# A two-layer decoder trunk: two squared blocks a layer taken pair by pair, the turn and the last stage rearranged

## The chip, the cores and the metric

One NeuronCore of one Trainium2 chip runs the whole kernel. The metric is the device time of one execution in microseconds, as the median of several runs. The profile is of one execution with its own time.

## What is computed

Two decoder layers over 256 rows of 2048 float32 values, weights streamed from HBM once. In words per layer (cut from the reference):

```python
a = rms_norm(x, n_mix_pre); proj = a @ w_in                  # 9760 columns
o_fox, o_nsa = fox_attention(...), nsa_attention(...)        # 8 + 8 heads of 128
mix = sigmoid(g_fox) * (o_fox @ w_up_fox) + sigmoid(g_nsa) * (o_nsa @ w_up_nsa)
x = x + rms_norm(mix @ w_out, n_mix_post)
a = rms_norm(x, n_ffn_pre)
h = (silu(a @ w_gate) * (a @ w_up)) @ w_down                 # hidden width 5632
x = x + rms_norm(h, n_ffn_post)
```

## The kernel before

The 256 rows are two halves of 128 (`t` = 0, 1). A float32 product is made as three TensorE products of rounded parts: high by high, high by low, low by high (`part`, `product`). The left operand is the transposed activation (`aT`, `hT`); the right operand is weights in units of 256 rows by 512 columns (432 in the first stage of a layer). A unit goes from HBM into one of 5 raw buffers by SP's DMA queue (`emit_raw`, L252), ScalarE rounds it to `wh` (L158) and VectorE subtracts that to give `wl` (L168): `split`. High and low parts live in 37 slots of 4 KB a partition, as do activations.

The program writes the order of each engine's instructions itself. `ensure(i)` is called ahead of each use of unit `i`: it emits splits up to `i`, and one more step of the next splits if the units alive stay within `room["slots"]` (set by `budget` and by the stages) and the look-ahead within `room["ahead"]`; with `room["slow"]` every second call does nothing more. `finish` gives slots back. `pump` after each unit advances one of up to two generators of side work (transposes, turns of the residual stream), which yield between their steps; `Once.need` drives one until it has yielded a key.

`chunk` makes 512 columns for both halves, unit by unit, half 0 and half 1 in turn. `skew=8` takes the last 8 units for half 0 first and then for half 1, so that half 0 is evacuated earlier; `on_t0` then starts its turn. `head=8` does the same with the first units.

`square_chunk` makes 512 columns of two weights (gate and up) or 1024 of one. Its first two pairs of units (`SEVEN = 2`) are taken with seven products in place of eight, over sums of blocks: `split_sums` makes the rounded sums in two steps (of 2 and 4 slot tiles), the left sums stand in `smh` and `sml`, and seven PSUM banks hold the products, each of three matmuls. With `together` the order is product by product, both pairs in each; without, pair by pair. `between` then combines the banks, and the remaining pairs follow in plain form. FFN blocks 2 to 10 of a layer are squared, with `together`; blocks 5 to 10 are the second part. `room["slots"]` is 14 in the down block ahead of block 5, and falls from 24 in block 5 to 14 in block 10 (L1281, L1368). The down products are squared too, pair by pair.

`tail` makes the last product of a stage (`out`, and the second part of `down`, which adds to partial sums `yg`), with `sum_evac`: add the partial sum (L604), square with row sums on ScalarE (L606), multiply by the norm's gains in place (L607). In `down` the first 1024 columns are one squared block of 12 pairs, then two chunks follow. `turn_gen` takes a half across to the next stage: the root from the row sums on POOL (`rstd_of`, L501 to L508), x plus scaled y in four pieces (L570), transposes into `aT` (`to_aT`), a copy of x to HBM. `end_gen` does the last stage and stores the output.

The program starts with `idle(6)`, six matmuls of zeros, while the first x comes in; `start_gen` transposes it.

Of the kernel before, what the change touches and what calls it, by code (L numbers as in the profile page):

```python
# [43 lines left out]
RAWS = 5  # L44
IDLE = (6, 1)
LAG = (3, 4)
KEPT = (1, 1)
ROOM_OUT = 10
ROOM_DOWN = 10

# [54 lines left out]
def trunk(ctx: ExitStack, tc: tile.TileContext, I: dict, consts: bass.AP, out: bass.AP):  # L105
# [68 lines left out]

    def load_x(src):
        xs = [[None, None], [None, None]]
        for t in range(2):
            for i in range(2):
                xs[t][i] = slot([128, 1024], F32, f"x{t}{i}")
                nc.sync.dma_start(xs[t][i], src[t * 128:(t + 1) * 128, i * 1024:(i + 1) * 1024])  # L180
        return xs

    gp = slot([128, 2, 128], F32, "gp")
# [254 lines left out]

    def square_chunk(pairs, lhs, sums, between, evac, before=None, together=True):

# [104 lines left out]
    def start_gen(t, xs, aT, rs, gcol):  # L545
        ss = small([128, 4], F32, "ss", 4)

        def rows(c):
            return xs[t][c // 2][:, (c % 2) * 512:(c % 2) * 512 + 512]

        for c in range(4):
            to_aT(aT, t, c, rows(c), gcol, True, t == 0 and c == 0)
            yield c
        for c in range(4):
            act.activation(junk, rows(c), AF.Square, accum_out=ss[:, c:c + 1])
            yield "sum"
        rs[t] = rstd_of(ss, "rs", True)
        yield "rs"

    def turn_gen(t, yg, ssy, xs, aT, rs, gcol, keep, lag):  # L560

        ry = rstd_of(ssy, "ry")
        yield "ry"
        ss = small([128, 4], F32, "ss", 4)

        def half(v, c):
            return v[t][c // 2][:, (c % 2) * 512:(c % 2) * 512 + 512]

        def add(c):
            dve.scalar_tensor_tensor(half(xs, c), half(yg, c), ry[:, 0:1], half(xs, c), op0=OP.mult, op1=OP.add)  # L570

        add(0)
        add(1)
        for _ in range(lag[t]):
            yield "add"
        for c in range(4):
            if c < 2:
                add(c + 2)
            to_aT(aT, t, c, half(xs, c), gcol)
            act.activation(junk, half(xs, c), AF.Square, accum_out=ss[:, c:c + 1])  # L580
# [8 lines left out]
    def end_gen(t, yg, ssy, xs):  # L589
        ry = rstd_of(ssy, "ry")  # L590
        for c in range(4):
            v = slice((c % 2) * 512, (c % 2) * 512 + 512)
            x, y = xs[t][c // 2][:, v], yg[t][c // 2][:, v]
            dve.scalar_tensor_tensor(x, y, ry[:, 0:1], x, op0=OP.mult, op1=OP.add)  # L594
            nc.sync.dma_start(out[0, t * 128:(t + 1) * 128, c * 512:(c + 1) * 512], x)
        yield "end"

    def sum_evac(yg, ssy, gb, c, partial):
        v = slice((c % 2) * 512, (c % 2) * 512 + 512)

        def go(t, p):
            y = yg[t][c // 2][:, v]
# [7 lines left out]
    def gain_rows(v):  # L610
        gb = [slot([128, 1024], F32, f"gb{i}") for i in range(2)]
        for i in range(2):
# [355 lines left out]
    def run_layer(l, P, aT, rs, turns, x_src, x_mid, x_next):  # L968
# [156 lines left out]


        xs = load_x(x_src)
        gb = gain_rows(I["norm_mix_post"][l])

# [10 lines left out]

        def tail(ids4, lhs, gb, xs, yg, partial, wait, gen):
            ssy = [small([128, 4], F32, "ssy", 4) for t in range(2)]
            turns = [None, None]

            def turn(t):
                turns[t] = Once(gen(t, yg, ssy[t], xs))
                waiting.append(turns[t])
# [3 lines left out]
            def between(ps):  # L1151

                y = [[yg[t][0][:, 512 * i:512 * i + 512] for i in range(2)] for t in range(2)]
                hu = staged([128, 2, 512], F32, "hu", 1)
# [8 lines left out]
                dve.tensor_tensor(y[1][1], y[1][1], hu[:, 0], op=OP.add)  # L1163

            for c in range(4):
                end = c == 3
                if ids4[c] is None:
                    continue
                if c == 2:
                    room["ahead"] = 11  # L1170
                if partial and c == 0:
                    ev = [sum_evac(yg, ssy, gb, i, partial) for i in range(2)]
                    square_chunk(ids4[0], lhs, lhs_s, between, lambda t, i, p: ev[i](t, p), wait, False)
# [11 lines left out]
        turns2 = tail(P["out"], lhs_m, gb, xs, y_rows(), False, wait_m,  # L1185
                      lambda t, yg, ss, xs: turn_gen(t, yg, ss, xs, aT2, rs2, g2, x_mid, LAG))
        del xs, gb
# [89 lines left out]
        def ffn(c):  # L1277
# [53 lines left out]

            square_chunk(P["ffn"][c], lhs_a2, lhs_s, between, evac)
            made_of(c, hb)
# [39 lines left out]
        hand_on()  # L1373
        xs = load_x(x_mid)
        gb = gain_rows(I["norm_ffn_post"][l])
        budget(ROOM_DOWN)
        if l + 1 < DEPTH:
            aT3, rs3 = [[None] * 4, [None] * 4], [None, None]
            g3 = (l + 1) * 16
            turns3 = tail(P["down"][1], lhs_h(b0), gb, xs, yg, True, wait_h(b0, b1),  # L1380
                          lambda t, yg, ss, xs: turn_gen(t, yg, ss, xs, aT3, rs3, g3, x_next, LAG))
            close_stage()
            return aT3, rs3, turns3
        tail(P["down"][1], lhs_h(b0), gb, xs, yg, True, wait_h(b0, b1), end_gen)
        drain()
# [69 lines left out]
```

## Time and profile before

| | |
|---|---|
| time, median of 3 runs | 2829.85 us (2827.48 to 2831.4) |
| the profiled execution | 2828.34 us, its span 2826.4 us |
| TensorE busy (matmul) | 2799.8 us, 99% of the span |
| VectorE, ScalarE, GpSimd (POOL) busy | 1937.1, 1409.2, 112.1 us |
| DMA | 547.04 MB, mean 194 GB/s |
| mean granted TensorE clock | 0.997 of full |

The span runs from the first to the last instruction of the profiled execution; its time has 1.9 us more. PE is TensorE, DVE VectorE, ACT ScalarE, SP SyncE's queue. Matmul ends are modelled and overlap the next start, so the distance from start to start says how long one takes in a stream. A bracket behind an instruction gives the idle time of its engine just before it and what ended it.

### The profile page before, as it was taken

The page shows a single profiled execution, that of the slowest core. Times are in us where ns is not written, and L with a number is a line of the kernel's source. Part 1 is how long each engine was busy: PE and PEld are TensorE (multiplying, and loading weights), DVE is VectorE, ACT ScalarE, POOL GpSimd, SP SyncE. Part 2 cuts the span into 40 slices and gives each one's busy share as a digit, 9 for nine tenths or more (in the row PEclk, how much of TensorE's full clock was granted, in tenths as well). Part 3 has the DMA queues.
Part 4 walks back from the last instruction along what each step waited for, and adds up shares of the span by engine and source line. Part 5 has one row for each costly group of instructions (what it writes and reads, how often), then busy time and mean ns, then how long its engine had stood idle before and what let it go on. Part 6 is the DMA issues. An engine that isn't in the chain of part 4 may idle for free. (4 is left out here: it accounts for less than half of the span.)

```text
span 2826.4 us, 35553 instructions
## 1 busy us (share of the span) xinstructions
PE 2799.8 (99%) x13134; PEld 2345.4 (83%) x13134; DVE 1937.1 (69%) x2485; ACT 1409.2 (50%) x1999; POOL 112.1 (4%) x190
## 2 busy tenths in 40 slices
PE   9999999999999999999999999999999999999998
PEld 8988888888888878878899888888888888788786
DVE  6666655556888788776666576655468886887755
ACT  6555554445554455454555455644465454555443
POOL 0100000001000000000011000000020000000000
PEclk9999999999999999999999999999999999999999
DMA  7674446575665565556566644455666655665564
GB/s 247 205 255 123 138 149 206 189 244 189 202 217 179 174 225 194 179 179 238 184 216 220 222 128 149 147 196 194 231 219 210 203 176 190 209 192 185 177 206 156
DMA packets 291807, 547.04 MB, mean 194 GB/s; under 512 B 17265, under 2 KB 59569, under 8 KB 291633
## 3 DMA queue, kind: packets, MB, share of 16 engines
q1 hardware_dynamic: 290000, 543.82, 58.6%
q8 instruction: 103, 1.69, 0.2%
q10 hardware_dynamic: 1632, 0.95, 0.1%
q14 instruction: 72, 0.58, 0.1%
HBM read 536.31 MB, written 8.39 MB: 193 GB/s over the span
## 5 line engine op out<-in xcount | busy, mean ns | idle before, releaser
L168 DVE TENSOR_TENSOR wl<-raw,wh 128x1024 fp32r<-128x1024 f32 (+1 forms) x912 | 1070.4, 1210 | 334.9 <-ACT wh L158 280.0
L158 ACT ACTIVATE wh<-raw 128x1024 fp32r<-128x1024 f32 (+1 forms) x1056 | 1059.3, 1044 | 459.2 <-DVE raw L272 129.2
L388 PE MATMUL acc<-wh,aT 128*128 128x512 f32 (+1 forms) x1534 | 597.9, 390 | 0.0
L390 PE MATMUL acc<-wh,aT 128*128 128x512 f32 (+1 forms) x1534 | 585.1, 381 | 0.9 <-DVE aT L542 0.9
L389 PE MATMUL acc<-wl,aT 128*128 128x512 f32 (+1 forms) x1534 | 584.8, 381 | 0.0
L435 PE MATMUL acc<-wh,aT 128*128 128x512 f32 x972 | 381.3, 392 | 0.0
L437 PE MATMUL acc<-wh,aT 128*128 128x512 f32 x972 | 378.8, 390 | 0.0
L436 PE MATMUL acc<-wl,aT 128*128 128x512 f32 x972 | 378.2, 389 | 0.0
L390 PEld LDWEIGHTS acc<-wh,aT 128*128 128x128 f32 x1534 | 287.9, 188 | 51.3 <-DVE aT L542 1.7
L388 PEld LDWEIGHTS acc<-wh,aT 128*128 128x128 f32 x1534 | 288.5, 188 | 44.0 <-issue 0.8
L389 PEld LDWEIGHTS acc<-wl,aT 128*128 128x128 f32 x1534 | 288.7, 188 | 41.5
L437 PEld LDWEIGHTS acc<-wh,aT 128*128 128x128 f32 x972 | 182.5, 188 | 38.4
L436 PEld LDWEIGHTS acc<-wl,aT 128*128 128x128 f32 x972 | 182.7, 188 | 37.0
L435 PEld LDWEIGHTS acc<-wh,aT 128*128 128x128 f32 x972 | 182.7, 188 | 36.8
L263 DVE TENSOR_TENSOR wl<-raw,wh 128x1024 fp32r<-128x1024 f32 x144 | 173.6, 1221 | 18.5 <-PE acc L436 9.2
L435 PE MATMUL acc<-wh,hT 128*128 128x512 f32 x452 | 176.9, 391 | 0.0
L437 PE MATMUL acc<-wh,hT 128*128 128x512 f32 x452 | 176.2, 390 | 0.0
L436 PE MATMUL acc<-wl,hT 128*128 128x512 f32 x452 | 175.9, 389 | 0.0
L388 PE MATMUL acc<-wh,oT 128*128 128x512 f32 x256 | 102.0, 399 | 0.0
L388 PE MATMUL acc<-wh,mixT 128*128 128x512 f32 x256 | 100.7, 393 | 0.0
L390 PE MATMUL acc<-wh,oT 128*128 128x512 f32 x256 | 99.9, 390 | 0.0
L390 PE MATMUL acc<-wh,mixT 128*128 128x512 f32 x256 | 99.7, 390 | 0.0
(333 smaller groups left out, 3295.7 us busy)
## 6 DMA issues: line engine op xcount, KB each, us to landing
raw<-in_w_in SPq DMA_DIRECT2D x224, 512.0 KB, 4.6
raw<-in_w_ffn_gate SPq DMA_DIRECT2D x176, 512.0 KB, 4.8
raw<-in_w_ffn_up SPq DMA_DIRECT2D x176, 512.0 KB, 4.6
raw<-in_w_ffn_down SPq DMA_DIRECT2D x176, 512.0 KB, 5.5
raw<-in_w_in SPq DMA_DIRECT2D x96, 432.0 KB, 4.4
raw<-in_w_out SPq DMA_DIRECT2D x64, 512.0 KB, 6.1
raw<-in_w_up_nsa SPq DMA_DIRECT2D x32, 512.0 KB, 4.7
raw<-in_w_up_fox SPq DMA_DIRECT2D x32, 512.0 KB, 4.6
```

The lines of the kernel that those rows point to most:

```text
L158: act.activation(o, i, AF.Copy, scale=1.0 if scale is None else scale)
L168: dve.tensor_tensor(lo, src, f32(hi), op=OP.subtract)
L263: dve.tensor_tensor(lo, src, f32(hi), op=OP.subtract)
L388: pe.matmul(ps[t][:, :n], ah, hi, start=first, stop=False)
L389: pe.matmul(ps[t][:, :n], ah, lo, start=False, stop=False)
L390: pe.matmul(ps[t][:, :n], al, hi, start=False, stop=end)
L435: pe.matmul(ps, ah, bh, start=first, stop=False)
L436: pe.matmul(ps, ah, bl, start=False, stop=False)
L437: pe.matmul(ps, al, bh, start=False, stop=last)
```

## The change

- FFN blocks 5 and 10 (the first and the last of the second part) go through `square_chunk` pair by pair (`together=False`).
- In `down`'s tail the multiplication by the gains is put off by one evacuation in the squared block; in the last chunk its result goes to a new tile `z`, and in the last layer half 1's go to PSUM banks. `skew` is 6 there (8 in `out`), `ROOM_DOWN` 9.
- The loads of x and of the gains move from before that squared block to its pair 5; the gains go into the tiles `smh` and `sml`, half 0's x into the tiles `wq`.
- The turn after `down` begins its first two adds in the step that makes the root (`prompt`); the turn after `out` does not.
- In the last stage of the program half 1's first quarter is scaled by ScalarE, added by GpSimd and stored from ScalarE's queue.
- `start_gen` has one more step between the second and third transposes; ten matmuls of zeros in place of six.

```diff
-IDLE = (6, 1)
+IDLE = (10, 1)
-ROOM_DOWN = 10
+ROOM_DOWN = 9
...
-    def square_chunk(pairs, lhs, sums, between, evac, before=None, together=True):
+    def square_chunk(pairs, lhs, sums, between, evac, before=None, together=True, load=None):
...
         for p in range(SEVEN, last + 1):
+            if load is not None and p == SEVEN + 3:
+                load()
...
             to_aT(aT, t, c, rows(c), gcol, True, t == 0 and c == 0)
             yield c
+            if c == 1:
+                yield "later"
...
+    def quarters(v):
+
+        return [[i[:, k:k + 512] for i in v[t] for k in (0, 512)] for t in range(2)]
...
+    def turn_gen(t, ys, ssy, xs, aT, rs, gcol, keep, prompt):
...
         ry = rstd_of(ssy, "ry")
-        yield "ry"
+        if not prompt:
+            yield "ry"
...
         add(0)
         add(1)
-        for _ in range(lag[t]):
+        for _ in range(LAG[t]):
             yield "add"
...
+    def end_gen(t, ys, ssy, xs):
         ry = rstd_of(ssy, "ry")
...
+        if t:
+
+            copy(act, ys[t][0], ys[t][0], ry[:, 0:1])
+            pool.tensor_tensor(x[0], ys[t][0], x[0], op=OP.add)
+            store(nc.scalar, 0)
+        for c in range(t, 4):
+            dve.scalar_tensor_tensor(x[c], ys[t][c], ry[:, 0:1], x[c], op0=OP.mult, op1=OP.add)
+            store(nc.sync, c)
         yield "end"
...
+    def sum_evac(ys, ssy, gb, c, partial, place):
...
             act.activation(junk, p, AF.Square, accum_out=ssy[t][:, c:c + 1])
-            dve.tensor_tensor(y, p, gb[c // 2][:, v], op=OP.mult)
+            ys[t][c] = place(t) or y
+
+            def times_gain():
+                dve.tensor_tensor(ys[t][c], p, gb[c // 2][:, v], op=OP.mult)
+            return times_gain
         return go
...
+            def place(c):
+
+                def of(t):
+                    if last and t and c:
+                        return bank(8 - c, "yb")
+                    return z[:, t] if partial and c == 3 else None
+                return of
+
             for c in range(4):
                 end = c == 3
+                if end and partial:
+                    z = slot([128, 2, 512], F32, "z")
...
+                    ev = [sum_evac(ys, ssy, gb, 0, True, place(0)), sum_evac(ys, ssy, gb, 1, True, place(1))]
+                    left = deque()
+
+                    def sums_of(t, i, p):
+                        left.append(ev[i](t, p))
+                        if len(left) > 1:
+                            left.popleft()()
+                    square_chunk(ids4[0], lhs, lhs_s, between, sums_of, wait, False, load)
+                    left.popleft()()
                 else:
-                    chunk(ids4[c], lhs, sum_evac(yg, ssy, gb, c, partial), skew=8 if end else 0,
+                    ev = sum_evac(ys, ssy, gb, c, partial, place(c))
+                    chunk(ids4[c], lhs, lambda t, p: ev(t, p)(), skew=0 if not end else 6 if partial else 8,
...
-            square_chunk(P["ffn"][c], lhs_a2, lhs_s, between, evac)
+            square_chunk(P["ffn"][c], lhs_a2, lhs_s, between, evac, together=c not in (b0, b1 - 1))
...
-        xs = load_x(x_mid)
-        gb = gain_rows(I["norm_ffn_post"][l])
+        xs, gb = [None, None], [None, None]
+
+        def load():
+
+            gb[:] = [staged([128, 1024], F32, nm, 1) for nm in ("smh", "sml")]
+            gain_rows(I["norm_ffn_post"][l], gb)
+            xs[:] = [[staged([128, 1024], F32, "wq") for i in range(2)], x_tiles(1)]
+            load_x(x_mid, xs)
+
         budget(ROOM_DOWN)
...
+                          lambda t, yg, ss, xs: turn_gen(t, yg, ss, xs, aT3, rs3, g3, x_next, True), load)
+            turns3[0].need("kept")
             close_stage()
```

## Rows read from the trace of the kernel before

**Rows 1.** The page, part 1: busy time and share of the span, each engine
```profile
PE 2799.8 (99%) x13134; PEld 2345.4 (83%) x13134; DVE 1937.1 (69%) x2485; ACT 1409.2 (50%) x1999; POOL 112.1 (4%) x190
```

**Rows 2.** The waits of PE: us in total, times, longest
```profile
PE acc L436 <- DVE wl L263: 9.8, 4, 2.8
PE acc L389 <- DVE wl L168: 0.9, 2, 0.4
```

**Rows 3.** The timeline at the start of blocks 5 and 10, layer 0
```profile
1015.39 0.40 PE L435 MATMUL acc<-wh,smh 128*128 128x512 f32 x1
1018.61 0.50 PE L436 MATMUL acc<-wl,smh 128*128 128x512 f32 x1 [2.11 <-DVE wl L263]
...
1233.07 0.40 PE L435 MATMUL acc<-wh,smh 128*128 128x512 f32 x1
1234.83 2.35 DVE L263 TENSOR_TENSOR wl<-raw,wh 128x1024 fp32r<-128x1024 f32 x2
1237.23 0.50 PE L436 MATMUL acc<-wl,smh 128*128 128x512 f32 x1 [2.78 <-DVE wl L263]
```

**Rows 4.** Windows of 20 us: busy (x), PEclk, DMA share, GB/s
```profile
1240.00:1260.00 20.00, 20.00 (x94) 16.56 (x93) 16.48 (x21) 9.49 (x11) 0.00 (x0) 1.00 0.57 185
2640.00:2660.00 20.00, 20.00 (x81) 16.29 (x82) 13.77 (x19) 6.89 (x9) 0.00 (x0) 0.86 0.47 153
2760.00:2780.00 20.00, 20.00 (x90) 16.57 (x89) 14.01 (x12) 11.69 (x11) 0.00 (x0) 1.00 0.95 325
```

**Rows 5.** The timeline as rows 0 to 127 turn, between the layers
```profile
1400.09 0.69 DVE L604 TENSOR_TENSOR yg<-acc,yg 128x512 f32<-128x512 f32 x1 [7.03 <-PE acc L390]
1401.78 0.68 POOL L504 TENSOR_SCALAR nw<-ssy,nw 128x1 f32<-128x1 f32 x1 [16.22 <-ACT junk L606]
1404.15 1.42 DVE L570 SCALAR_TENSOR_TENSOR x<-yg,ry,x 128x512 f32<-128x512 f32 x2 [1.83 <-POOL ry L508]
1405.34 0.60 PE L493 MATMUL tp<-ct,x 128*128 128x128 f32 x4
```

**Rows 6.** The timeline as rows 128 to 255 turn, between the layers
```profile
1410.82 1.05 DVE L168 TENSOR_TENSOR wl<-raw,wh 128x864 fp32r<-128x864 f32 x1
1415.47 0.68 DVE L604 TENSOR_TENSOR yg<-acc,yg 128x512 f32<-128x512 f32 x1
1417.91 1.38 POOL L505 TENSOR_TENSOR nw<-nw,warm 128x1 f32<-128x1 f32 x1
1421.47 0.66 PE L493 MATMUL tp<-ct,x 128*128 128x128 f32 x4 [0.53 <-DVE x L570]
1425.00 0.46 PE L390 MATMUL acc<-wh,aT 128*128 128x432 f32 x1 [0.86 <-DVE aT L542]
```

**Rows 7.** The timeline of DVE after the squared block of the tail
```profile
1348.77 0.69 DVE L607 TENSOR_TENSOR yg<-yg,gb 128x512 f32<-128x512 f32 x1 [0.85 <-ACT junk L606]
```

**Rows 8.** The timeline of PE in the first 15 us
```profile
1.17 2.74 PE L1413 MATMUL idle<-junk 128*128 128x512 bf16 x6 [1.17 <-DVE warm L189]
4.83 0.63 PE L493 MATMUL tp<-ct,x 128*128 128x128 f32 x4 [0.92 <-DMA x<-in_x]
14.69 0.95 PE L493 MATMUL tp<-ct,x 128*128 128x128 f32 x4 [1.12 <-DVE aT L542]
```

**Rows 9.** The timeline of the last stage
```profile
2816.18 0.69 DVE L604 TENSOR_TENSOR yg<-acc,yg 128x512 f32<-128x512 f32 x1 [4.07 <-PE acc L390]
2820.22 2.74 DVE L594 SCALAR_TENSOR_TENSOR x<-yg,ry,x 128x512 f32<-128x512 f32 x4 [1.81 <-POOL ry L508]
```

**Rows 10.** Groups of POOL by line and shape: busy, mean ns
```profile
L519 POOL TENSOR_TENSOR ropea<-kskw,ct 128x128 f32<-128x128 f32 x4 | 1.9, 463 | 108.2 <-ACT kskw L158 108.0
L520 POOL TENSOR_TENSOR ropeb<-kskw,ct 128x64 f32<-128x64 f32 x4 | 1.3, 326 | 0.0
L522 POOL TENSOR_TENSOR ropeb<-nq,ct 128x128 f32<-128x128 f32 x4 | 5.8, 1447 | 0.0
```

**Rows 11.** The waits of SyncE's DMA queue: us in total, times, longest
```profile
SPq L252 <- DVE wl L168: 1862.3, 885, 18.1
```

More of the change, by code (lines that the diff above doesn't have):

```diff
@@ L173, in trunk, with load_x, x_tiles @@
     x_in = I["x"][0]
-    def load_x(src):
-        xs = [[None, None], [None, None]]
+    def load_x(src, xs):
         for t in range(2):
             for i in range(2):
-                xs[t][i] = slot([128, 1024], F32, f"x{t}{i}")
                 nc.sync.dma_start(xs[t][i], src[t * 128:(t + 1) * 128, i * 1024:(i + 1) * 1024])
         return xs
+    def x_tiles(t):
+        return [slot([128, 1024], F32, f"x{t}{i}") for i in range(2)]
     gp = slot([128, 2, 128], F32, "gp")
@@ L578, in turn_gen @@
                 add(c + 2)
-            to_aT(aT, t, c, half(xs, c), gcol)
-            act.activation(junk, half(xs, c), AF.Square, accum_out=ss[:, c:c + 1])
+            to_aT(aT, t, c, x[c], gcol)
+            act.activation(junk, x[c], AF.Square, accum_out=ss[:, c:c + 1])
             yield c
@@ L587, in turn_gen, with store @@
         yield "rs"
-    def end_gen(t, yg, ssy, xs):
+    def end_gen(t, ys, ssy, xs):
         ry = rstd_of(ssy, "ry")
[L591 to L595, printed above, removed]
+        x = quarters(xs)[t]
+        def store(queue, c):
+            queue.dma_start(out[0, t * 128:(t + 1) * 128, c * 512:(c + 1) * 512], x[c])
+        if t:
[3 more added lines that the diff above has]
+        for c in range(t, 4):
+            dve.scalar_tensor_tensor(x[c], ys[t][c], ry[:, 0:1], x[c], op0=OP.mult, op1=OP.add)
+            store(nc.sync, c)
         yield "end"
-    def sum_evac(yg, ssy, gb, c, partial):
+    def sum_evac(ys, ssy, gb, c, partial, place):
         v = slice((c % 2) * 512, (c % 2) * 512 + 512)
         def go(t, p):
-            y = yg[t][c // 2][:, v]
+            y = ys[t][c]
             if partial:
@@ L606, in go, with gain_rows @@
             act.activation(junk, p, AF.Square, accum_out=ssy[t][:, c:c + 1])
-            dve.tensor_tensor(y, p, gb[c // 2][:, v], op=OP.mult)
-        return go
-    def gain_rows(v):
-        gb = [slot([128, 1024], F32, f"gb{i}") for i in range(2)]
+            ys[t][c] = place(t) or y
+            def times_gain():
+                dve.tensor_tensor(ys[t][c], p, gb[c // 2][:, v], op=OP.mult)
+            return times_gain
+        return go
+    def gain_rows(v, gb):
         for i in range(2):
@@ L1124, in run_layer @@
         close_stage()
-        xs = load_x(x_src)
-        gb = gain_rows(I["norm_mix_post"][l])
+        xs = load_x(x_src, [x_tiles(t) for t in range(2)])
+        gb = gain_rows(I["norm_mix_post"][l], [slot([128, 1024], F32, f"gb{i}") for i in range(2)])
         def lhs_m(t, kt):
@@ L1139, in y_rows, with tail @@
             return [[slot([128, 1024], F32, f"yg{t}{i}") for i in range(2)] for t in range(2)]
-        def tail(ids4, lhs, gb, xs, yg, partial, wait, gen):
+        def tail(ids4, lhs, gb, xs, yg, partial, wait, gen, load=None, last=False):
+            ys = quarters(yg)
             ssy = [small([128, 4], F32, "ssy", 4) for t in range(2)]
@@ L1145, in turn @@
             def turn(t):
-                turns[t] = Once(gen(t, yg, ssy[t], xs))
+                turns[t] = Once(gen(t, ys, ssy[t], xs))
                 waiting.append(turns[t])
@@ L1151, in between @@
             def between(ps):
-                y = [[yg[t][0][:, 512 * i:512 * i + 512] for i in range(2)] for t in range(2)]
+                y = ys
                 hu = staged([128, 2, 512], F32, "hu", 1)
@@ L1185, in run_layer @@
         turns2 = tail(P["out"], lhs_m, gb, xs, y_rows(), False, wait_m,
-                      lambda t, yg, ss, xs: turn_gen(t, yg, ss, xs, aT2, rs2, g2, x_mid, LAG))
+                      lambda t, yg, ss, xs: turn_gen(t, yg, ss, xs, aT2, rs2, g2, x_mid, False))
         del xs, gb
@@ L1380, in run_layer @@
             turns3 = tail(P["down"][1], lhs_h(b0), gb, xs, yg, True, wait_h(b0, b1),
-                          lambda t, yg, ss, xs: turn_gen(t, yg, ss, xs, aT3, rs3, g3, x_next, LAG))
+                          lambda t, yg, ss, xs: turn_gen(t, yg, ss, xs, aT3, rs3, g3, x_next, True), load)
+            turns3[0].need("kept")
             close_stage()
             return aT3, rs3, turns3
-        tail(P["down"][1], lhs_h(b0), gb, xs, yg, True, wait_h(b0, b1), end_gen)
+        tail(P["down"][1], lhs_h(b0), gb, xs, yg, True, wait_h(b0, b1), end_gen, load, True)
         drain()
```

8 lines of the change are left out of this document (2 added, 6 removed).

## The prediction

> **What bounds the kernel now.** I read the page first: TensorE is busy 99% of the span and no other engine comes near [rows 1]. The change adds four small matmuls and removes none, so it can win only where TensorE stands still, where its clock is low, and after its last matmul. The second view was therefore the list of what TensorE waits for: one wait carries most of it, the products of a squared block (L436) waiting for low halves that VectorE subtracts at L263, four times, 9.8 us [rows 2]. The third was the timeline at those four places: the first matmuls of FFN blocks 5 and 10, in both layers. In each the first product of pair 0 runs (three matmuls), then the same product of pair 1 begins and its second matmul waits [rows 3]. The fourth was a table of windows, for the granted clock: it is 1.00 after the stall of block 10 in layer 0, and 0.86 over 20 us after the same stall in layer 1 [rows 4]. The last was the timeline of the turn between the layers, the tail's evacuations, the start and the end [rows 5 to 9].
>
> **Blocks 5 and 10 (together=False).** Now both pairs are wanted within four matmuls. Matmuls in a block start 0.23 us apart (some 88 begin in the undisturbed window [rows 4]). Block 5: from its first matmul at 1015.39 to the released one at 1018.61 are 3.22 us for four starts, 0.92; lost 2.30. Block 10: 1233.07 to 1237.23, 4.16, lost 3.24 [rows 3]. The waits of both layers add up to twice these two (9.8 against 2.11 + 2.78 [rows 2, 3]), so the four cost 2 x 5.54 = 11.1 us. In the new order all seven products of pair 0, 21 matmuls or 4.83 us, stand ahead of pair 1. VectorE's queue there does not change: the second step of pair 1's split is emitted at the head of the block in both orders, by `ensure`, behind the same evacuations. In block 10 VectorE works on it from 1234.83 to 1237.18; pair 1's low half is first wanted at 1233.07 + 4.83 + 0.23 = 1238.1. In block 5 it is ready by 1018.6 and wanted at 1020.4 [rows 3]. So the cover is 0.9 us in block 10 and 1.8 in block 5, and the stalls go whole: **-11.1**. Bounds: 0 (another wait takes the place of each) and -11.1. What is late next: the sums in `between` start after product 1, with 9 matmuls (2.1 us) behind it in place of 18; the bank of product 1 is written again only 18 matmuls later still, so 6.2 us cover a copy and four adds of about 0.7 each (L604, one pass of 512 [rows 5]). `ensure` is called four times in the head in place of nine, but pair 0's slots come free 4.8 us after the start, and pair 2 is wanted after 42 matmuls, 9.7 us. I cost both at nothing.
>
> **The clock.** [...] It follows the stall of block 10 in layer 1, so without the stall I take **-2.8**; bounds 0 and -2.8. The stall of equal length in layer 0 was not followed by it. [...]
>
> **Evacuations of the tail's squared block.** The multiplication by the gains (L607) overwrites what ScalarE still squares, so VectorE waits 0.85 us each of four times [rows 7], and the splits queued behind it make TensorE wait 0.4 us once a layer, 0.9 in all [rows 2]. With the multiplication put off by one evacuation, VectorE needs 8 passes of 0.69, 5.5 us, without those waits, and the splits come 2 us or more earlier: **-0.9**, bounds 0 and -0.9.
>
> **Loads of x and gains.** They move from before the tail's squared block to its sixth pair, on SP's queue among the weights; six loads of 512 KB at 325 GB/s [rows 4] take 9.7 us. Behind them wait the weight loads, and for these the splits. SP stands waiting for a free raw buffer for 1862 us of the span [rows 11], so five loads (and up to four split units) lie ahead: nine units of 12 matmuls at 0.23, 25 us. 9.7 is under that: 0.
>
> **The turn between the layers.** TensorE now loses 0.53 (transposes wait for x) and 0.86 (a matmul waits for the low half of aT) [rows 6], 1.4. With skew 6 and the adds issued at once, the first transposes of half 0 stand behind 3 units in place of 4 (one step of the turn, after the row sums, is dropped). From the evacuation at 1400.09 x is ready at 1404.86, 4.8 us [rows 5]; POOL's step at L504 then no longer runs beside L607, which I take as 0.3 less (half of its 0.68), so 4.5. Three units are 18 matmuls, 4.1 us; with the hand-over some 0.6 us are missing. For half 1 VectorE now issues the adds ahead of the next splits, and waits for POOL without working. It evacuated half 1 15.4 us after half 0 [rows 5, 6]; with one split (1.05) less before it I take 14.0, x at 14.0 + 4.5 = 18.5. TensorE wants it after 6 units, four transposes of 0.36, the stall of 0.6 and 6 units of the next layer (432 columns, 12 x 0.195 or less, half of them for half 0: 1.18 each): 8.2 + 1.4 + 0.6 + 7.1 = 17.3. Missing: 1.2. The seventh unit's split follows the two adds (14.0 + 5.2 + 1.05 = 20.3) and is wanted at 18.5 + 0.4 + 0.2 = 19.1: another 1.1. The 0.86 goes, since one more unit, with its transposes 1.5 us, lies between the transposes and their use. Sum 0.6 + 1.2 + 1.1 = 2.9 against 1.4: **+1.5**. Bounds: -1.4 (all gone) and +4.9 (these stalls grow by a split of 1.05 each way and draw the 2.8 of the clock).
>
> **Start.** [...] The step put between the second and third transposes lets six matmuls that are ready (12 with the half after them) run where TensorE waits 1.12 for VectorE to empty a bank [rows 8]. I take **-1.1**; bounds +0.9 and -1.3.
>
> **Last stage.** Half 1's four adds, 2.74 us [rows 9], become three, 0.69 less. The fourth goes over ScalarE (taken as VectorE's pass of 512, 0.69 [rows 7]) and POOL: 64 more elements cost 463 - 326 = 137 ns [rows 10], so 512 take 463 + 6 x 137 = 1.29 us; 1.98 against VectorE's 2.05: both end together. The two last stores then leave at one moment and share the way, so I count half of 0.69, and 0.3 for L504 as in the turn: **-0.6**. If POOL were held up as in its slow row (1447 against 463 for the same shape [rows 10]), its add would take up to 4.0 us and, at 0.69 + 4.0, end 2.0 after VectorE's old 2.74; less the 0.3 that is +1.7. The other bound is -1.0. [...]
>
> **Sum.** 11.1 + 2.8 + 0.9 + 1.1 + 0.6 - 1.5 = 15.0. From the profiled execution's 2828.34 (span 2826.4 and 1.9 around it) this gives 2813.3; that execution lies 1.5 under the median of the three runs, which would give 2814.8. I forecast **2814**.
>
> **The rivals.** What a measurement can tell from no change is 0.2%, 5.7 us.
> A. *The block stalls move.* Some 1 to 1.5 us stay in each of blocks 5 and 10, because pair 1's or pair 2's split falls behind (the cover in block 10 is only 0.9). For it: that cover; against it: the tail's squared blocks already run pair by pair and appear in no wait [rows 2]. 15.0 - 4 x 1.5 = 9.0, or 6.2 with the clock still falling once: 2819 to 2822. Chance 0.13.
> B. *The turn pays double.* Its stalls reach 4 us and the clock falls there: 4.9 in place of 1.5: 2818. For it: VectorE idles twice on POOL with next-layer splits behind it. Chance 0.16.
> C. *The turn wins.* POOL, undisturbed by splits (its L505 took 1.38 at 1417.91 beside them [rows 6]), answers early and no stall is left: 15.0 + 2.9 = 17.9: 2811. Chance 0.14.
> D. *Slower: SP's queue is held in the tail.* The loads of half 1's x wait for two free slots, and every weight load stands behind them. Up to 25 us less 9.7, some 15 us of waiting, TensorE sees nothing; beyond that each us costs one in each of two layers. The kernel is slower by 0.2% when both lose 10.4, a wait of some 26 us: 2836. Before, six slots were asked for there, now two. Chance 0.03.
> E. *The change does little.* The splits and not the order bound these blocks, so most of the 11.1 comes back as waits at pair 2: 2824 to 2832. Against it: VectorE has 1.8 us of idle time ahead of the adds elsewhere [rows 5], and TensorE's list has no other wait for splits of over 0.2 us than the two of [rows 2]. Chance 0.07.
>
> **How the numbers follow.** The forecast has 0.47, for 2812.5 to 2817. With B and C and most of A the range is 2807.5 to 2822, which leaves D, E and the edges out, under 2 in 10. Faster by over 0.2% (under 2824.2) are forecast, A, B, C and a little of E: 0.91. Within: most of E: 0.05. Slower: D and a rest: 0.04.
>
> **What would show it.** The wait of L436 for L263 gone from TensorE's list, and no wait in the 42 matmuls of blocks 5 and 10; granted clock 1.00 in the window after block 10 of layer 1; L389 without its wait after the tail's squared block; three waits in the turn, of 0.6 for half 0's transposes and about 1 each for half 1's and the seventh unit; no 1.12 at the start; POOL's add near 1.3 us, ending with VectorE's third. The prediction is wrong if TensorE waits at pair 2 of those blocks, or for raw loads in the tail.

## The result and the profile after

The changed kernel takes 2813.73 us (median of 6 executions, 2812.95 to 2815.08) against 2829.02 (6 executions, 2827.48 to 2831.4): a ratio of 0.9946, 95% interval 0.9933 to 0.9959. Faster, as forecast, and 0.3 us from the forecast time. The profiled execution took 2813.84 us, its span 2812.0, 14.4 less than before.

The page of the changed kernel, part 1, answers to [rows 1]. TensorE's busy time fell by 3.4 us, though it runs four matmuls more; its mean granted clock is 0.999, before 0.997.

```profile
PE 2796.4 (99%) x13138; PEld 2343.2 (83%) x13138; DVE 1935.9 (69%) x2484; ACT 1408.8 (50%) x2000; POOL 110.3 (4%) x191
```

The waits of PE, changed kernel (us in total, times, longest), against [rows 2]. Lines have moved: L436 of before is L437 here, L389 is L390, L263 is L264.

```profile
PE tp L496 <- DVE aT L545: 0.9, 1, 0.9
PE acc L390 <- DVE wl L168: 0.8, 1, 0.8
PE tp L496 <- DVE x L579: 0.8, 1, 0.8
PE acc L399 <- ACT wh L158: 0.6, 1, 0.6
PE tp L496 <- DVE wq L579: 0.4, 1, 0.4
...
PE acc L437 <- DVE wl L264: 0.3, 1, 0.3
```

The wait of 9.8 us is gone. What is left of that pair of lines, 0.3 us, stands in another block (the tail's). The two waits after the tail's squared block are gone too; lines 1 and 4 are the start's, lines 2, 3 and 5 are the turn's. The windows of 20 us that answer to [rows 4] (busy (x), PEclk, DMA share, GB/s): the clock after block 10 of layer 1 is 1.00 for 0.86.

```profile
1240.00:1260.00 20.00, 20.00 (x94) 16.56 (x93) 16.49 (x21) 11.11 (x13) 0.00 (x0) 1.00 0.63 210
2640.00:2660.00 20.00, 20.00 (x92) 16.57 (x91) 16.31 (x19) 12.71 (x14) 0.00 (x0) 1.00 0.64 208
```

TensorE runs the same 11,568 matmuls into tiles `acc`, in places in another order within a block. The start of the n-th of them in one trace less that in the other says how far a kernel leads there; the difference over a stretch is what the stretch won.

| stretch | won, us | predicted |
|---|---|---|
| start (to 92 us) | 0.13 | 1.1 |
| block 5, layers 0 and 1 | 2.29, 2.32 | 2.30 each |
| block 10 of layer 0, with the first products of the tail | 2.92 | 3.24 |
| block 10 of layer 1, with the clock | 5.95 | 6.04 |
| first products of the tail, layer 1 | -0.49 | 0 |
| evacuations of the tail's squared block, layers 0 and 1 | 0.75, 0.73 | 0.45 each |
| turn between the layers | -0.78 | -1.5 |
| after the last of these matmuls | 0.43 | 0.6 |

The rest of the span's 14.4 us lies in stretches of 0.1 and less. Between executions of programs that are alike up to a point, these leads differ by 0.1 to 0.5 us, at the start above all, and there once by 1.5 (the first experiment, whose start is that of before); the stretch of -0.49 is -0.15 in the one other execution of a program that is the same up to there (the end on VectorE, below).

Three places, from the timeline of the changed kernel. First the head of block 10, layer 0, which answers to [rows 3]. The block's first matmul is at 1230.48; pair 1's second step of the split ends at 1234.6, and its low half is wanted at 1235.61, by the second of its matmuls.

```profile
1230.48 0.40 PE L436 MATMUL acc<-wh,smh 128*128 128x512 f32 x1
1232.24 2.35 DVE L264 TENSOR_TENSOR wl<-raw,wh 128x1024 fp32r<-128x1024 f32 x2
1235.61 0.39 PE L437 MATMUL acc<-wl,smh 128*128 128x512 f32 x1
```

Then the first products of the tail's squared block in layer 0: the same two operations meet here, and now TensorE is first. The second fence gives the windows of that place (PE, PEld, DVE, ACT, POOL busy): VectorE, the third figure, is busy for 9.6 of 10 us.

```profile
1276.83 2.35 DVE L264 TENSOR_TENSOR wl<-raw,wh 128x1024 fp32r<-128x1024 f32 x2
...
1278.71 0.40 PE L436 MATMUL acc<-wh,smh 128*128 128x512 f32 x1
1279.23 0.50 PE L437 MATMUL acc<-wl,smh 128*128 128x512 f32 x1
```

```profile
1265.00:1275.00 10.00, 10.00 (x46) 8.26 (x45) 9.67 (x14) 4.56 (x7) 0.00 (x0) 1.00 0.32 107
1275.00:1285.00 10.00, 9.87 (x43) 7.75 (x42) 9.61 (x12) 6.05 (x7) 0.00 (x0) 1.00 0.47 138
```

Then the turn, against [rows 5, 6]:

```profile
1396.61 0.69 DVE L623 TENSOR_TENSOR yg<-acc,yg 128x512 f32<-128x512 f32 x1 [11.81 <-PE acc L391]
1398.30 0.27 POOL L507 TENSOR_SCALAR nw<-ssy,nw 128x1 f32<-128x1 f32 x1 [24.98 <-ACT junk L625]
1400.25 1.42 DVE L579 SCALAR_TENSOR_TENSOR wq<-yg,ry,wq 128x512 f32<-128x512 f32 x2 [2.23 <-POOL ry L511]
...
1410.53 0.68 DVE L623 TENSOR_TENSOR yg<-acc,yg 128x512 f32<-128x512 f32 x1
1414.14 1.42 DVE L579 SCALAR_TENSOR_TENSOR x<-yg,ry,x 128x512 f32<-128x512 f32 x2 [2.21 <-POOL ry L511]
1414.95 0.66 PE L496 MATMUL tp<-ct,x 128*128 128x128 f32 x4 [0.76 <-DVE x L579]
1415.47 2.99 DVE L168 TENSOR_TENSOR wl<-raw,wh 128x864 fp32r<-128x864 f32 x3
1416.58 0.46 PE L390 MATMUL acc<-wl,aT 128*128 128x432 f32 x1 [0.78 <-DVE wl L168]
```

From the evacuation to the adds are 3.64 and 3.61 us (before 4.06 in half 0); VectorE idles 2.2 us twice on POOL, and the three splits stand behind the adds.

### The profile page after: what moved, and what is told of

The parts are those of the page before. It is cut to its first block, busy times and chain, and to the rows that moved or that the text cites. A ratio compares the mean times of both kernels' runs of the same rounds, so it can differ in the third digit from the quotient of the medians.

```text
span 2812.0 us, 35564 instructions
## 1 busy us (share of the span) xinstructions
PE 2796.4 (99%) x13138; PEld 2343.2 (83%) x13138; DVE 1935.9 (69%) x2484; ACT 1408.8 (50%) x2000; POOL 110.3 (4%) x191
## 3 DMA queue, kind: packets, MB, share of 16 engines
q8 instruction: 103, 1.69, 0.2%
## 4 chain that ended last, share of the span: by engine, by line
PE 96%; DVE 2%; DMA 1%; ACT 1%; issue 1%; POOL 0%; SPq 0%; DVEq 0%; ACTq 0%; POOLq 0%
PE acc L389 18%; PE acc L391 17%; PE acc L390 17%; PE acc L438 12%; PE acc L437 12%; PE acc L436 12%; PE hT L496 1%; PE ph L828 1%; PE ph L827 1%; PE tp L496 0%; PE ns L653 0%; PE ns L652 0%; PE no L646 0%; PE no L645 0%; PE no L647 0%
## 5 line engine op out<-in xcount | busy, mean ns | idle before, releaser
L389 PE MATMUL acc<-wh,aT 128*128 128x512 f32 (+1 forms) x1534 | 597.9, 390 | 0.0
L390 PE MATMUL acc<-wl,aT 128*128 128x512 f32 (+1 forms) x1534 | 584.9, 381 | 0.8 <-DVE wl L168 0.8
L436 PE MATMUL acc<-wh,aT 128*128 128x512 f32 x972 | 381.5, 392 | 0.0
L437 PE MATMUL acc<-wl,aT 128*128 128x512 f32 x972 | 378.2, 389 | 0.0
L389 PEld LDWEIGHTS acc<-wh,aT 128*128 128x128 f32 x1534 | 288.4, 188 | 43.8 <-issue 0.8
L390 PEld LDWEIGHTS acc<-wl,aT 128*128 128x128 f32 x1534 | 288.7, 188 | 42.6 <-DVE wl L168 1.1
L437 PEld LDWEIGHTS acc<-wl,aT 128*128 128x128 f32 x972 | 182.7, 188 | 37.1
L436 PEld LDWEIGHTS acc<-wh,aT 128*128 128x128 f32 x972 | 182.5, 188 | 36.9
L264 DVE TENSOR_TENSOR wl<-raw,wh 128x1024 fp32r<-128x1024 f32 x144 | 173.6, 1221 | 17.6 <-PE acc L437 8.3
L436 PE MATMUL acc<-wh,hT 128*128 128x512 f32 x452 | 176.8, 391 | 0.0
L437 PE MATMUL acc<-wl,hT 128*128 128x512 f32 x452 | 175.9, 389 | 0.0
L389 PE MATMUL acc<-wh,oT 128*128 128x512 f32 x256 | 102.0, 399 | 0.0
L389 PE MATMUL acc<-wh,mixT 128*128 128x512 f32 x256 | 100.7, 393 | 0.0
L438 PEld LDWEIGHTS acc<-wh,hT 128*128 128x128 f32 x452 | 84.8, 188 | 17.9
```

Of the source, the lines that this page charges most:

```text
L264: dve.tensor_tensor(lo, src, f32(hi), op=OP.subtract)
L389: pe.matmul(ps[t][:, :n], ah, hi, start=first, stop=False)
L390: pe.matmul(ps[t][:, :n], ah, lo, start=False, stop=False)
L436: pe.matmul(ps, ah, bh, start=first, stop=False)
L437: pe.matmul(ps, ah, bl, start=False, stop=False)
L438: pe.matmul(ps, al, bh, start=False, stop=last)
```

## The experiments

Times are medians, with the lowest and the highest; a ratio is to the kernel before on the same chip, with its 95% interval.

**1. Is it the order inside blocks 5 and 10?** The kernel before with this one line of the change:

```diff
-            square_chunk(P["ffn"][c], lhs_a2, lhs_s, between, evac)
+            square_chunk(P["ffn"][c], lhs_a2, lhs_s, between, evac, together=c not in (b0, b1 - 1))
```

> The kernel before with the pair-by-pair order in FFN blocks 5 and 10 and nothing else of the change. Theory M (the order of the two pairs is what TensorE waited on): the four waits of L436 for L263 vanish, TensorE is 2.3 us earlier behind block 5 and 3.2 behind block 10 of a layer, 2.8 more behind block 10 of layer 1 where the clock no longer falls; about 0.3 to 0.5 comes back at the tail's squared block in each layer. Sum 13 us, 2816. Rival S (the splits are the bound, and the gain came from slots and loads freed in the tail): the waits move into the same blocks, gain under 4 us, 2825 or more.

2816.22 us (2815.31 to 2816.81), ratio 0.9953, interval 0.9939 to 0.9968. The wait at L436 is gone from the list; blocks 5 win 2.29 and 2.31, block 10 of layer 0 wins 3.23. The rest of the list is that of before, with 0.9 after the tail's squared block and 1.9 for 1.1 at the start. I had expected 0.3 to 0.5 us a layer to come back at the tail's squared block, and that was wrong: 0.0 and 0.07 did. There VectorE ends pair 1's second step at 1280.34, 0.36 us before TensorE takes it, and in layer 1 0.13 before; in the kernel before it was 1.0 in both layers.

```profile
1277.98 2.36 DVE L263 TENSOR_TENSOR wl<-raw,wh 128x1024 fp32r<-128x1024 f32 x2
1280.70 0.39 PE L436 MATMUL acc<-wl,smh 128*128 128x512 f32 x1
```

So this one line carries most of the change; all the other edits together are worth some 2.5 us.

The changed kernel without it (`together` left at its default in all blocks), and with block 5 alone in pairs (`together=c != b0`):

> The changed kernel with blocks 5 and 10 taken product by product again. Theory M: the four waits of 2.1 to 2.8 us are back, 2826 to 2827 in executions in which the clock falls once, 2823 to 2824 in those in which it does not. Rival S: under 2817.

> The changed kernel with block 10 alone back to product by product, block 5 pair by pair. Theory M: two waits of 2.8 us at block 10, none at block 5; TensorE 3.2 us later behind block 10 in each layer, less 0.3 to 0.5 that the tail's squared block no longer waits: 2819 to 2820, and 2822 where the clock falls after block 10. Rival C (the clock fell because of something else in layer 1, as the tail's loads): granted clock stays at 1.00 throughout, 2819.5, never more. Rival S: 2814 to 2815.

The first: 2826.92 us (2825.35 to 2829.83), ratio 0.9993, 0.9983 to 1.0002; the four waits are back, 9.8 us. The second came out slower than any of the three theories said: 2824.94 (2822.0 to 2827.09), ratio 0.9984, 0.9975 to 0.9994. Waits of PE of both, the first fence that of the first:

```profile
PE acc L437 <- DVE wl L264: 9.8, 4, 2.8
```

```profile
PE acc L437 <- DVE wl L264: 5.6, 2, 2.8
PE acc L390 <- DVE wl L168: 2.7, 1, 2.7
```

With block 5 alone in pairs there is a new wait of 2.7 us, in the turn. The timeline there:

```profile
1418.90 3.96 DVE L168 TENSOR_TENSOR wl<-raw,wh 128x864 fp32r<-128x864 f32 x4
1420.00 0.73 PE L390 MATMUL acc<-wl,aT 128*128 128x432 f32 x1 [2.72 <-DVE wl L168]
```

Four splits stand behind the adds, in place of three: one unit of the next layer fewer was split ahead. `ensure` counts its calls and, in the turn, skips every second one by the parity of that count; a block in pairs calls it a different number of times, so one block changed alone shifts the parity and two leave it. That is read from the code and fits the fourth split; no run set the parity by itself.

**2. What takes the clock down?** The windows of both runs. The first fence is the kernel with all blocks product by product, at block 5 and block 10 of layer 0 and at block 10 of layer 1; the second is the one with block 5 alone in pairs, at block 10 of layer 0, the turn, and block 10 of layer 1. The share of the clock is the third figure from the end.

```profile
1010.00:1030.00 20.00, 17.89 (x71) 14.22 (x70) 15.37 (x17) 11.12 (x12) 0.00 (x0) 0.91 0.59 204
1230.00:1250.00 20.00, 17.21 (x69) 13.47 (x68) 14.55 (x19) 6.78 (x8) 0.00 (x0) 0.91 0.41 133
2635.00:2655.00 20.00, 17.21 (x78) 13.68 (x78) 15.16 (x21) 8.23 (x10) 0.00 (x0) 1.00 0.37 131
```

```profile
1230.00:1250.00 20.00, 17.20 (x72) 13.51 (x71) 14.86 (x20) 7.31 (x9) 0.00 (x0) 0.91 0.40 133
1415.00:1435.00 20.00, 17.28 (x81) 15.94 (x80) 13.80 (x28) 14.38 (x37) 11.09 (x20) 0.83 0.41 142
2635.00:2655.00 20.00, 17.20 (x72) 13.45 (x71) 14.71 (x20) 7.28 (x9) 0.00 (x0) 0.91 0.40 131
```

Behind the same stall of block 10 in layer 1 the clock fell in the profile of before (0.86 [rows 4]) and in the second run here (0.91), not in the first (1.00); behind that of layer 0 it fell in both runs (0.91) and not before (1.00). How far it fell, the kernel before shows within the window of 0.86:

```profile
2640.00:2645.00 5.00, 5.00 (x12) 3.86 (x13) 2.49 (x3) 0.00 (x0) 0.00 (x0) 0.50 0.96 338
```

There matmuls start 0.43 us apart, where 0.23 is usual. So in these windows it is not that place but the stall that the fall follows, and not every time. The new wait in the turn was followed by it as well (0.83; behind that wait matmuls of 432 columns start 0.36 us apart, ahead of it 0.19): that run lost 3.8 us more in the turn than the changed kernel. Over 47 executions of the kernel before the mean clock was 0.995 to 0.999, and the span went from 2823.8 us (mean of three at 0.999) to 2831.1 (two at 0.995); all six of the changed kernel were at 0.999, spans 2811.2 to 2813.3.

**3. The turn.** The adds of both halves, or of half 1, again one step behind POOL's root:

```diff
-        if not prompt:
-            yield "ry"
+        yield "ry"
```

```diff
-        if not prompt:
+        if t or not prompt:
```

> The changed kernel, but between the layers each half's rows scale (ry) again comes one step of the order before the adds, instead of in the same step. Theory T (the turn's +0.8 us is the price of taking the adds at once: the transposes of half 0 wait 0.4 us, those of half 1 0.8 us and the seventh unit's split 0.8 us behind VectorE, which stands at the adds until POOL's scale is there): those waits become near those of the kernel before, the turn gives back 0.8 to 1.6 us, time 2812.2 to 2813.0 us. Rival U (the turn's loss comes from the skew of 6 and from the order of the splits, not from the adds): the same waits stay or grow, time 2813.7 to 2815.5 us.

> The changed kernel, but only half 0 takes its adds at once; half 1's scale again comes one step before its adds. Theory T: half 0's wait of 0.4 us stays, those of half 1 (0.8 us at the transposes, 0.8 us at the seventh unit's split) shrink by 0.8 to 1.6 us together; time 2812.2 to 2813.0 us, about that of the run in which neither half does. Rival U: no gain, 2813.7 to 2815.5 us.

2812.85 (2812.36 to 2813.59; ratio 0.9944, 0.9926 to 0.9962) and 2812.92 (2812.51 to 2813.09; the same ratio). Both medians are below all six times of the changed kernel; on their chip a variant that differs from it in the last 7 us alone (the end on VectorE, below) took 2813.54. Without any prompt add the turn itself wins 1.3 us over the changed kernel (its first loses 0.78 against before, this wins 0.52), with the prompt in half 0 alone 0.58. Of its waits, half 1's transposes keep 0.4 and the seventh unit's split 0.2 in the first; in the second the transposes keep 1.1 and the split none. So the turn lost by the adds taken at once: the two traces show that. That the medians lie 0.8 to 0.9 us below the changed kernel's agrees, but with six and four executions, whose times overlap, it is no more than likely. But of the 1.69 us that the first of these leads by at block 10 of layer 1, 0.93 is gone after the tail's first products, where its timeline has

```profile
2674.34 0.40 PE L436 MATMUL acc<-wh,smh 128*128 128x512 f32 x1
2675.89 0.50 PE L437 MATMUL acc<-wl,smh 128*128 128x512 f32 x1 [1.15 <-DVE wl L264]
```

**4. The tail: multiplication by the gains at once, and who sets its start.**

```diff
                         left.append(ev[i](t, p))
-                        if len(left) > 1:
-                            left.popleft()()
+                        left.popleft()()
                     square_chunk(ids4[0], lhs, lhs_s, between, sums_of, wait, False, load)
-                    left.popleft()()
```

> The changed kernel, but after the tail's squared block each quarter's norm weights are multiplied in at once, as before the change, instead of one quarter later. Theory V (the matmuls after that block wait on the last quarter's add, which stands behind the multiplications on VectorE, 0.7 us less so for the change): a wait of 0.4 to 0.8 us returns behind the block in both layers, time 2814.5 to 2815.3 us. Rival (the 0.7 us per layer came from somewhere else, the earlier loads or z): no change, 2813.7 us within 0.5.

2814.91 (2814.21 to 2815.15), ratio 0.9951, 0.9935 to 0.9967: a wait of 0.4 us is back in each layer, and the stretch costs 0.73 and 0.74 more. In its timeline of PE the wait of 0.43 shows; from start to start are 0.82 us where 0.23 is usual, and the matmul that waited is long as well.

```profile
1344.24 0.39 PE L389 MATMUL acc<-wh,hT 128*128 128x512 f32 x1
1345.06 0.50 PE L390 MATMUL acc<-wl,hT 128*128 128x512 f32 x1 [0.43 <-DVE wl L168]
```

In `split_sums`, for the pairs of the tail's squared block, one of the four sums given to GpSimd, with a split of VectorE's, `low(gh, gl, rg)`, put behind it from ahead of the sums (cut; `g` is marked as `tail` for these pairs alone):

```diff
-        low(gh, gl, rg)
+        if not g.get("tail"):
+            low(gh, gl, rg)
...
-        dve.tensor_tensor(ru[:, 0], ru[:, 0], rg[:, 0], op=OP.subtract)
+        if g.get("tail"):
+            pool.tensor_tensor(ru[:, 0], ru[:, 0], rg[:, 0], op=OP.subtract)
+            low(gh, gl, rg)
+        else:
+            dve.tensor_tensor(ru[:, 0], ru[:, 0], rg[:, 0], op=OP.subtract)
```

> The changed kernel, but in the tail's squared block one of the four sums of each of the seven pairs of weight units is GpSimd's instead of VectorE's, with a split of VectorE's meanwhile. Theory B (what comes back at the start of the tail's squared block, 0.3 us in layer 0 and 0.5 us in layer 1, is VectorE, which is busy 9.6 of 10 us there): each pair relieves VectorE by 0.69 us less a wait of about 0.3 us for GpSimd, these two waits shrink or go, time 2813.0 to 2813.4 us. Rival P (an add of GpSimd's out of SBUF and VectorE's work beside it hold each other up): VectorE's instructions grow by about what GpSimd's take, the waits grow to 1 to 2 us, time 2814.5 to 2816 us.

> Both at once: neither half takes its adds at once (2812.85 us by itself, where 0.9 of the 1.7 us that layer 0 and the turn had won came back as a wait at the tail's squared block of layer 1), and one sum of each pair there is GpSimd's. Theory B: that wait of 1.1 us shrinks to 0.3 to 0.7, time 2812.0 to 2812.6 us. Rival (the wait is set by when the weights come in, not by VectorE): 2812.9 us, the wait stays at 1.1. Rival P: 2814 us or more.

The first is the changed kernel with this edit, the second the version without prompt adds with it. There are two such pairs a layer, not seven as I wrote. 2818.96 (2817.03 to 2821.43; 0.9967, 0.9953 to 0.9981) and 2816.71 (2815.18 to 2818.13; 0.9957, 0.9942 to 0.9972): both slower than without. A group of POOL, an instruction of VectorE beside it and a wait of VectorE, all of the first:

```profile
L275 POOL TENSOR_TENSOR raw<-raw 128x512 f32<-128x512 f32 x4 | 8.6, 2149 | 1108.4 <-DMA raw<-in_w_ffn_down 559.9 <-DVE raw L273 548.4
```

```profile
1270.22 1.22 DVE L264 TENSOR_TENSOR wl<-raw,wh 128x1024 fp32r<-128x1024 f32 x1
```

```profile
DVE raw L279 <- POOL raw L275: 4.7, 4, 1.2
```

GpSimd's subtraction took 2.15 us, and VectorE, relieved of 0.69, waited 1.2 for it, each time. Its own split beside it stayed at 1.22 us, so rival P is half right: of the two only GpSimd's grew, against the 1.27 us of its add of the same size in the last stage. TensorE's waits there grew to 1.7 and 1.9 us. So VectorE came later, by 1.0 us a layer from these rows, and TensorE with it, by 1.6 in layer 0 and 1.9 in layer 1 against the changed kernel: this was no relief, and the delay went through in full. In the second run TensorE lost 1.7 and 4.0, by the same measure; there the clock fell behind the wait in layer 1 (0.91 over 2670 to 2690 us, 1.00 in the first run; the mean 0.998 and 0.999). What the rest of the loss is made of (ScalarE's copies wait for the sums too) was not taken apart. That relief for VectorE would win there, theory B, was so neither shown nor ruled out.

One buffer more for raw weights, one slot less for split ones, on top of the version without prompt adds:

```diff
-SLOTS = 37
-RAWS = 5
+SLOTS = 36
+RAWS = 6
```

> The version without the adds at once (2812.85 us by itself), with six buffers for raw weights instead of five, paid for by one slot of split weights fewer (36 for 37). Ahead of the tail's squared block of layer 1 VectorE waits 4.5 us in all, between 2647 and 2658 us, for splits whose raw weights land late, and is then busy 9.7 of 10 us. Theory B, carried one step back: with a sixth buffer the loads start earlier, these waits shrink, and the wait of 1.1 us at the tail's squared block shrinks to 0.5 or less; time 2812.0 to 2812.5 us. Rival (one slot fewer lets fewer units be split ahead, everywhere): waits for weights appear in other places, time 2814 us or more.

2832.39 (2830.4 to 2834.41), ratio 1.0011, 1.0002 to 1.0021. The rival's sign, waits in other places, and a time far above its bound. Waits of PE

```profile
PE acc L437 <- DVE wl L264: 7.1, 4, 2.8
PE acc L436 <- ACT wh L158: 5.2, 2, 2.6
```

in each layer at the head of one FFN block (in layer 0 between 1160 and 1215 us, a block that had none) and at that of the tail's squared block. The granted clock was 0.91 in the 20 us around each of the four places, and 0.995 to 0.997 over the whole of each of the eleven executions. That one slot fewer lets less be split ahead fits; the sixth buffer by itself was not run, and whether earlier loads would help VectorE there can't be seen behind that, and stays open.

**5. Start and end.** Six zeros again (`IDLE = (6, 1)`); no extra step in `start_gen` (the two lines `if c == 1: yield "later"` out); the last stage's four adds and stores on VectorE and SP alone (`for c in range(4)`, without the branch `if t`).

> The changed kernel with six zeros first, as before. Theory Z (the four zeros put the first transposes off and eat what the extra step of the start wins): the first transposes start at 4.8 in place of 5.4, and by 33 us TensorE is 0.5 to 1.1 us ahead of the changed kernel; 2813.0. Rival W (the zeros keep the clock up between 7 and 11 us): the granted clock is 0.50 there as before, and by 33 us TensorE is level or up to 0.5 us behind; 2814.0.

> The changed kernel without the extra step (later) in the first gains of a half at the start, so that the third and fourth transposes of a half come one step earlier, as before the change; the ten zeros stay. Theory: the wait for aT of 0.87 us at 20 us goes back to 14.7 us and is 1.0 to 1.4 us, the first 33 us cost 0.2 to 0.5 us more, time 2813.9 to 2814.3 us. Rival (the step only moves the wait and is worth nothing): 2813.7 us within 0.2.

> The changed kernel, but the last half's four adds and stores are again VectorE's and SP's alone. The last add then ends one add (0.69 us) later; by the predicted step the store way that all share takes back half of it. Theory: the end is 0.3 to 0.7 us later, time 2814.0 to 2814.5 us. Rival (the last store is bound by its own way, not by the adds): within 0.15 us of the changed kernel.

Six zeros: 2813.49 (2812.51 to 2814.07; 0.9944, 0.9929 to 0.9959). It leads the changed kernel by 0.47 us at 33 us, and has given all but 0.06 back at the tail of layer 0, where the wait for L264 grew; the net is nothing. No extra step: 2814.52 (2813.54 to 2816.24; 0.995, 0.9935 to 0.9965), with this wait in place of 0.87 us at 20 us:

```profile
14.59 0.95 PE L496 MATMUL tp<-ct,x 128*128 128x128 f32 x4 [1.52 <-DVE aT L545]
```

In its profile this costs 0.06 us by 33 us against the changed kernel's profile, and 0.1 to 0.5 against four others with that kernel's start. In the profile of the kernel before with blocks 5 and 10 in pairs (six zeros, no extra step) the same wait was 1.94 us and the four transposes behind it took 0.85 us up to the next start, where before and here they took 0.71; that start lost 1.5 us against the one of before; two of the four executions here had a mean clock of 0.998, in place of 0.999. That the step spares such executions fits this, and was not shown.

The end on VectorE: 2813.54 (2813.35 to 2814.12; 0.9947, 0.9931 to 0.9962), no loss. From the last of the matmuls to the end are 10.26 us, 10.23 in the changed kernel and 10.66 before. The last stage of the changed kernel:

```profile
2803.91 0.26 POOL L507 TENSOR_SCALAR nw<-ssy,nw 128x1 f32<-128x1 f32 x1 [4.74 <-ACT junk L625]
...
2805.85 0.72 ACT L158 ACTIVATE yg<-yg,ry 128x512 f32<-128x512 f32 x1 [2.11 <-POOL ry L511]
2805.85 2.07 DVE L611 SCALAR_TENSOR_TENSOR x<-yb,ry,x 128x512 f32<-128x512 f32 x3 [2.20 <-POOL ry L511]
...
2806.64 1.27 POOL L608 TENSOR_TENSOR x<-yg,x 128x512 f32<-128x512 f32 x1 [0.83 <-ACT yg L158]
2807.94 0.38 ACTq L603 DMA_DIRECT2D out<-x  x1
```

and with the end on VectorE:

```profile
2803.41 0.26 POOL L507 TENSOR_SCALAR nw<-ssy,nw 128x1 f32<-128x1 f32 x1 [4.74 <-ACT junk L620]
...
2805.35 0.75 DVE L606 SCALAR_TENSOR_TENSOR x<-yg,ry,x 128x512 f32<-128x512 f32 x1 [2.20 <-POOL ry L511]
2806.02 2.06 DVE L606 SCALAR_TENSOR_TENSOR x<-yb,ry,x 128x512 f32<-128x512 f32 x3
```

From the first add to the end are 6.2 us in all three kernels, with four adds or three. The stores' 1.05 MB move from 1.6 to 4.6 or 4.8 us after the first add, at 330 to 400 GB/s and a DMA share of 1.0: their bytes, and not the number of adds, set it. What the end won is POOL's first step, 0.26 us where before it took 0.68, as in the turn [rows 5]; both versions have that.

## Why the prediction was right, and where it was off

*Blocks 5 and 10 (-11.1), right in mechanism and size.* Counted from start to start, not by the wait shown: predicted 2.30 and 3.24, measured 2.29 and 2.31 for blocks 5 and 3.23 for block 10 of layer 0, in the kernel before with this line alone. The cover in block 10, the time by which the split is ready before it is wanted, was 1.0 us, predicted 0.9.

*"I cost both at nothing"*: the four `ensure` calls in place of nine cost nothing in the blocks; but what the sum left out is the tail's first products, 0.4 us in layer 0 and 0.15 to 0.5 in layer 1. Before, VectorE caught up while TensorE stood in block 10 and was 1.0 us early one block on; now it does not catch up, and is late there. That is rival A's mechanism, at another place and a small part of its price. The line alone does not bring it: with it VectorE was still 0.36 and 0.13 us early. But TensorE was 1.5 us late from the start on in that profile, and the tail's loads and slots were those of before; which of these makes up the rest was not separated.

*The clock (-2.8)*: right for the profiled execution (5.95 less the 3.23 of the stall leave 2.7). The 2.8 is what a window of 20 us at 0.86 [rows 4] falls short of one at 1.00, an estimate. The two sets of windows above show that at one place, behind the same stall, the fall comes in one execution and not in another. So 2.8 was one execution's price, not the kernel's: the mean span of the changed kernel's six executions is 2812.1; that of before is 2823.8 in three at 0.999, 11.7 more, and 2827.6 in 23 at 0.997, 15.5 more.

*Evacuations of the tail (-0.9)*: 1.5 measured, and 1.5 lost again when it was undone. The step that failed is taking the waits of [rows 2] as the loss. A wait of 0.4 us cost 0.7 from start to start; the blocks I had counted from start to start, and these not.

*Loads of x and the gains (0)*: no wait for them shows, and rival D's held queue did not come; nothing was run on it alone.

*The turn (+1.5)*: +0.8. Its three waits are where they were put, 0.4, 0.8 and 0.8 us (predicted 0.6, 1.2, 1.1), and half 1 was evacuated 13.9 us after half 0 (14.0). From start to start they cost 0.6, 0.9 and 1.0, 2.5 in all, so near 2.9; but before, counted alike, cost 1.7 and not 1.4. The cause, adds that hold VectorE for POOL, is shown by the run without them, which wins 1.3 us there; rival C, with no stall left, would have won 2.2 (1.4 over before, and 0.8). Rival B's price was paid in one experiment, where one more split stood there and the clock fell: 4.6 us.

*Start (-1.1)*: 0.1 to 0.6 over nine profiles of programs with this same start, against the one profile of before. The first experiment has the start of before too and lay 1.5 us behind that profile at 33 us; against it the same start won 1.6 to 2.1. So how much the start is worth in the mean stays open. The upper bound, +0.9, has the four zeros at the 0.46 us each of [rows 8]; the -1.1 has them at almost nothing, which no run shows. With six in place of ten TensorE was 0.47 us ahead at 33 us (fifth group of runs). The ten start 0.43 us apart (1.17 to 5.42), no faster than the six before:

```profile
1.17 4.45 PE L1464 MATMUL idle<-junk 128*128 128x512 bf16 x10 [1.17 <-DVE warm L190]
5.42 1.06 PE L496 MATMUL tp<-ct,x 128*128 128x128 f32 x4
...
20.08 0.96 PE L496 MATMUL tp<-ct,x 128*128 128x128 f32 x4 [0.87 <-DVE aT L545]
```

The transposes are 0.6 us late against [rows 8], and the wait of 1.12 did not go but moved to 20 us as 0.87.

*Last stage (-0.6)*: 0.43, all of it POOL's step (0.42, where I had 0.3). Half of 0.69 for the fourth add was wrong: the shared store way took all of it back. POOL's add ran as worked out, 1.27 us for 1.29, and ended with VectorE's third. That it would not be held up (the bound of +1.7) was my estimate, and no row of before shows it. The run has VectorE's adds beside it with one input in PSUM; where VectorE's split, with both inputs in SBUF, ran beside the first 1.0 us of it, in the fourth group of runs, GpSimd's subtraction of the same size took 2.15.

The sum held by some luck, since errors of both signs met in it: too hopeful by 1.0 at the start, 0.9 at block 10 and the tail's first products and 0.2 at the end; too careful by 0.6 in the evacuations and 0.7 in the turn.

## What to carry to other kernels

Price a stall from start to start of the instructions around it, before and after alike; the wait that a list shows left out up to half of the loss here. Where a stall on one engine goes, ask whether another used it to catch up: here up to 0.5 us of the gain came back one block later, and so did most of one further gain ahead of it (fewer zeros) and part of another (the turn without prompt adds), since VectorE, and not TensorE, set when that block's second pair began. The gain of the prompt in half 0 alone stayed. Edits to an order written out by hand depend on each other through what is counted along it: one of the two blocks changed alone won less than its share and put a stall in a stage that the edit does not touch.

## What the runs showed of the hardware

- Behind a wait of TensorE of 2.8 us at the head of block 10 the granted clock of the 20 us windows fell in some executions and not in others at the same place: in layer 0 1.00 in the kernel before and 0.91 in both runs of the second question, in layer 1 0.86, 1.00 and 0.91. Behind one of 1.9 at the tail's squared block of layer 1 it was 0.91 in the second run with the sum on GpSimd, and 1.00 in the first. In the window of 0.86 it was 0.50 over 2640 to 2645 us, with matmuls 0.43 us apart for 0.23. The changed kernel, which has none of these waits, held a mean of 0.999 in all six.
- GpSimd's add of 128x512 in float32 took 1.27 us beside VectorE's adds with an input in PSUM (last stage of the changed kernel). Its subtraction of that size took 2.15 (mean of four) where a VectorE split with both inputs in SBUF, which stayed at 1.22, ran beside its first 1.0 us.
- A POOL step on one column took 0.26 and 0.27 us with VectorE idle (changed kernel, 2803.91 and 1398.30) and 0.68 beside a VectorE multiplication with both inputs in SBUF (before, 1401.78 [rows 5] and 2817.87).
